# Modulation columns in twos, the first chunk's layer norm in a chained order, a pair's down weights one tile sooner: a two-layer trunk on one core

## The chip, the cores and the metric

The kernel runs on one core of one Trainium2 chip, in one launch. The metric is the device time in microseconds; before the change the median of three runs is 1838.02 us (1836.39 to 1839.01). The profile is of one further execution. Five engines work side by side, each through its own list of instructions in order: TensorE (PE in the profile, its weight loads PEld), VectorE (DVE), ScalarE (ACT), GpSimd (POOL) and SyncE (SP), which issues most DMAs. They meet through semaphores only.

## The reference

The trunk has two layers. x is 1024 tokens by 1024 channels, float32; D_FF is 2816.

```python
def conformer_conv(h, w1, b1, w_dw, b_dw, ln_g, ln_b, w2, b2):
    u = h @ w1 + b1
    a, g = jnp.split(u, 2, axis=-1)
    u = a * jax.nn.sigmoid(g)
    u = lax.conv_general_dilated(u, w_dw...)          # causal, width 31, each channel by itself
    u = jax.nn.silu(layer_norm(u + b_dw, ln_g, ln_b))
    return u @ w2 + b2
...
def reference(x, c, ...):
    c_act = jax.nn.silu(c)
    for i in range(DEPTH):                            # 2
        mod = c_act @ ada_w[i] + ada_b[i]
        sh_m, sc_m, g_m, sh_f, sc_f, g_f = jnp.split(mod, N_ADA, axis=-1)
        h = modulate(rms_norm(x, norm_mix_g[i]), sh_m, sc_m)
        y = conformer_conv(h, ...) if i == 0 else multiscale_pool(h, ...)
        x = x + (1.0 + g_m)[:, None, :] * y
        h = modulate(rms_norm(x, norm_ffn_g[i]), sh_f, sc_f)
        y = (silu(h @ w_gate) * (h @ w_up)) @ w_down
        x = x + (1.0 + g_f)[:, None, :] * y
    return rms_norm(x, final_g)
```

multiscale_pool takes, for each of four groups of 256 channels, the trailing mean over 2, 4, 8 or 16 tokens minus the token itself, and then a 256 x 256 product.

## The kernel before

x lies transposed, 128 channels on the partitions, in eight tiles (k = 0 to 7) of two chunks of 512 tokens, A (`ch.i` 0) and B. Each float32 product is made of three matmuls: weights and activations are split into a high part (`hi`, a cast to a shorter mantissa) and the rest (`lo`), and hi·hi, lo·hi and hi·lo are summed in PSUM. A "product" below is one such matmul, 128x128 by 128x512. For a weight tile SP loads `raw`; ScalarE casts it to its high half (`CAST w<-raw`) and writes its negative (`ACTIVATE w<-raw`), and GpSimd issues a second DMA that adds the weight from memory onto the latter (`POOL DMA_DIRECT2D w<-in_...`), which leaves the low half. A tile of 128x1024 serves 24 products (8 k times 3).

The order of the instructions on the engines is set while the program is written out. The products come in units (`unit`, `run_units`), and between them a planner (`pace`) advances tasks, which are Python generators, as far as an estimated clock of TensorE allows: a `yield "load"` holds a task back for `LOAD["load"]` us of TensorE's time, and `stretch[0]` scales the estimated times of VectorE and GpSimd. So a number in these tables moves instructions of all engines.

The stages: start-up until 68 us; until 244 us the conv input products `a` and `g` of A, then of B. Meanwhile VectorE and ScalarE with GpSimd do the 31 taps of the depthwise convolution (`ca` on VectorE, `pr` on ScalarE and `pa` on GpSimd), ScalarE squares x of chunk B (`acc<-x`, `t<-x`) for its norm, and the task `ada_columns` makes the modulation's columns j = 2 to 5: 32 tiles `adaw` of 512 KB, in two buffers (`ADA_BUFS`), each used by four small matmuls `ada`. From 228 to 258 us stands the layer norm with silu of A: `mean` on TensorE, subtraction and squares, `var` on TensorE, a reciprocal root in twelve small VectorE instructions (`var`, `col`), `rstd` on TensorE (it spreads the root over the partitions), then for each k a multiplication by rstd (VectorE), silu (ScalarE, into `t`), the cast `vhi` and the rest `vlo`, which the products `y` of conv_out read. Then the FFN of layer 0. The pool mixer of layer 1 (`pool_mixed`: window sums `win`, halves `mxhi` and `mxlo`) runs beside FFN products, at about 960 to 1010 us for one chunk and 1340 to 1380 us for the other. In each of three FFN stretches (from about 780, 1156 and 1523 us) `ffn_mixed` uses pairs: class `Pair` makes sums of two weight tiles, class `Downs` fetches the down weights (`raw<-in_wdn_dram`) of the tiles before. ScalarE and VectorE need a `raw` tile before a pair's products can start.

The list `before` of `ffn_mixed` holds the units that run ahead of the pairs, and the planner walks it in order.

Of the kernel before, what the change touches and what calls it, by code (L numbers as in the profile page):

```python
# [9 lines left out]
F32 = mybir.dt.float32  # L10
# [9 lines left out]
KT = D // P  # L20
# [17 lines left out]
ADA_BUFS = 2  # L38
# [8 lines left out]
PHTAPS = 29  # L47
PHLEN = 135
OUT_B = 3
LOAD = {"load": 2.5, "slow": 18.0, "next": 4.0}  # L50
AHEAD = 4
STRETCH = 1.35
LATER = 300
WARM = (22, 10, 6)
# [58 lines left out]
def trunk(ctx, tc, xT, c, vec, ada, adan, w1, w2, wgu, wdn, wpl, wph, out):  # L113
# [37 lines left out]
    def either(n):  # L151

        now = clock["PE"]
        v, g = (max(clock[e], now) + engines[e].price("tensor_tensor", n) for e in "VG")
        return V_ if v <= g else G_
# [13 lines left out]

    tasks = []  # L170
    lax = [False]
    stretch = [1.0]
    forced = [False]

    def step(t, e):
# [61 lines left out]
    def slot(ch, name, dt=F32R):  # L237

        return slots.tile([P, ch.n], dt, tag=f"s{ch.i}", name=nm(name))
# [22 lines left out]
    def temp(n, name="t", bufs=0):  # L262
        t = tmp.tile([P, TMPW], F32, tag=name if bufs else "t", name=nm(name), bufs=bufs or 4)
        return t[:, :n]
# [47 lines left out]
    def ada_load(src):  # L312
        w = raws.tile([P, D], F32, tag="ada", name=nm("adaw"), bufs=ADA_BUFS)
        sync.dma_start(w, src)
        return w
# [43 lines left out]
    def ada_columns(js):  # L359


        todo = [(j, k) for j in js for k in range(KT)]
        src = lambda j, k: adan[k, :, (j - 2) * D : (j - 1) * D]
        ws = [ada_load(src(*t)) for t in todo[:ADA_BUFS]]
        for i, (j, k) in enumerate(todo):
            yield "load"
            if k == 0:
                acc = bank("ada")
            w = ws.pop(0)
            for g in range(4):  # L370
                matmul(acc[32 * g : 32 * g + 32, :Q], ccols[:, k, :], w[:, g * Q : g * Q + Q], start=k == 0, stop=k == KT - 1)
            clock["PE"] -= 1.3
            if i + ADA_BUFS < len(todo):
                ws.append(ada_load(src(*todo[i + ADA_BUFS])))
            if k == KT - 1 and (j == 2 or not held[0]):
                yield from columns_done(j, acc)
            elif k == KT - 1:
                held_back.append((j, acc))
# [348 lines left out]
    def centred(vs, mean, n):  # L727
# [7 lines left out]
                V_.tensor_tensor(vs[k], vs[k], mean, op=SUB)  # L735
        yield

    def layer_norm_silu(ch):

        n = ch.n  # L740
        vs = [st["u", ch.i, k][:, HALO:] for k in range(KT)]
        acc = temp(n, "acc", 2)
        for k in range(1, KT):
            while not (st["taps", ch.i][k - 1] and st["taps", ch.i][k]):
                yield "wait"
            V_.tensor_tensor(acc, vs[0] if k == 1 else acc, vs[k], op=ADD)
            yield
        yield "stats"
        b = bank("mean")
        matmul(b, ones, acc, start=True, stop=True)  # L750
        if ch.i == 0:
            yield from centred(vs, b, n)
        else:
            for k in range(KT):
                V_.tensor_tensor(vs[k], vs[k], b, op=SUB)
                yield
        acc = yield from sum_sq([vs[k] for k in CENTRED], n)
        rstd = yield from mean_rsqrt(acc, n)
        S_.activation(tmp.tile([P, 16], F32, tag="col0", name=nm("col"), bufs=1)[:, 0:1], acc[:, 0:1], AF.Silu)
        hv = [(slot(ch, "vhi"), slot(ch, "vlo")) for _ in range(KT)]  # L760
        for k in range(KT):
            V_.tensor_tensor(vs[k], vs[k], rstd, op=MUL)
            sw = temp(n)
            S_.activation(sw, vs[k], AF.Silu, bias=V("conv_ln_b", k), scale=V("conv_ln_g", k))
            hi, lo = hv[k]
            if ch.i == 0 and k % 2 == 0:
                V_.tensor_copy(hi, sw)
            else:
                S_.copy(hi, sw)
            (either(n) if ch.i else (G_, V_)[k % 2]).tensor_tensor(lo, sw, hi.bitcast(F32), op=SUB)  # L770
            yield
        st["v", ch.i] = hv

# [47 lines left out]
    def pool_mixed(ch, k):  # L821

        w = WINDOWS[k // (KT // len(WINDOWS))]
        h = st["hp", ch.i][k]
        n = ch.n
        end = PHALO + n
        bufs = [window(end, "win") for _ in range(2 if w > 2 else 1)]
        cur, have, i = h, 1, 0
        while have < w:
            first = PHALO - (w - 2 * have)  # L830
            nxt = bufs[i % 2]
            either(n).tensor_tensor(nxt[:, first:end], cur[:, first:end], cur[:, first - have : end - have], op=ADD)
            cur, have, i = nxt, have * 2, i + 1
            yield
        f = PHALO
        if ch.i == 0:
            f = PHALO + w - 1
            head = cur[:, PHALO:f]
            G_.tensor_tensor(head, head, recip[:, : w - 1], op=MUL)
            G_.tensor_tensor(head, head, h[:, PHALO:f], op=SUB)  # L840
        V_.scalar_tensor_tensor(cur[:, f:end], cur[:, f:end], 1.0 / w, h[:, f:end], op0=MUL, op1=SUB)
        hi, lo = st["mx", ch.i, k] = slot(ch, "mxhi"), slot(ch, "mxlo")
        S_.copy(hi, cur[:, PHALO:end])
        yield
        V_.tensor_tensor(lo, cur[:, PHALO:end], hi.bitcast(F32), op=SUB)

# [288 lines left out]
    def ffn_mixed(ch, l, until, at_end=False):  # L1135

        before = []
        for f in range(0, PLAIN, 2):
            before += [ffn_p1(ch, l, f, True, False), ffn_p1(ch, l, f + 1, True, False)]
            if f:  # L1140
                before.insert(-1, ffn_p2(ch, l, [f - 2, f - 1], True))
        mates = [Pair(ch, l, f, which) for f in range(PLAIN, until, 2) for which in range(2)]
        mine, theirs = [None] * len(mates), []
        for i, f in enumerate(range(PLAIN - 2, until - 2, 2)):
            first, second = Downs(ch, l, (f, f + 1), (0, 1)), Downs(ch, l, (f, f + 1), (2, 3))
            for at, d in ((2 * i + 1, first), (2 * i + 2, second)):
                if at < len(mates):
                    mine[at] = d
                else:
                    theirs.append(d)  # L1150
        last, = theirs
        paired = [(lambda take: mates[0].prepare(), ())]
        for i, me in enumerate(mates):
            if i + 1 == len(mates):
                paired.append((lambda take: reserve.__setitem__(0, 2), ()))
            paired.append(ffn_pair(ch, l, me, mates[i + 1] if i + 1 < len(mates) else None, mine[i], (mine + [last])[i + 1]))
        paired.append((lambda take: last.load(last.dps[1]), ()))
        rest = ffn(ch, l, True, at_end, until, ffn_p2(ch, l, [until - 2, until - 1], True))
        rest[1:1] = [alone(last)]
        return before, paired, rest  # L1160
# [388 lines left out]
```

## Time and profile before

| | us |
| --- | --- |
| median of 3 runs | 1838.02 (1836.39 to 1839.01) |
| the profiled execution | 1835.9 |
| its span | 1834.0 |
| TensorE busy | 1784.8 |
| VectorE busy | 1310.7 |
| ScalarE busy | 1040.0 |
| GpSimd busy | 587.8 |

In the tables below, `out<-in` names what an instruction writes and reads, `x8` how many instructions a row groups, and `[7.76 <-DMA adaw<-in_adan_dram]` says that the engine stood idle for 7.76 us ahead of it until that DMA was done. Rows begin with their start in us and their length. In a table by stretch the columns are the length, then busy time with number of instructions for TensorE, its weight loads, VectorE, ScalarE and GpSimd, then TensorE's granted clock, the DMA engines' share and GB/s.

### The profile page before, as it was taken

What the parts mean: (1) busy time and instruction counts of PE and PEld (TensorE: products, weight loads), DVE (VectorE), ACT (ScalarE), POOL (GpSimd) and SP (SyncE); (2) the same over time, 40 slices, a digit from 0 to 9 for tenths busy, and PEclk for the clock granted to TensorE, in tenths of its full rate; (3) what the DMA queues carried; (4) which work ended last, traced back from release to release, by engine and by line L of the source; (5) the groups of instructions that cost most, each with busy time, mean ns of one, the idle gap of its engine ahead of it and who ended that gap; (6) DMA issues with size and microseconds to landing.
All of it is one profiled execution on the core that took longest, in us unless ns stands there. A gap on an engine that the chain in (4) does not pass through costs nothing.

```text
span 1834.0 us, 26261 instructions
## 1 busy us (share of the span) xinstructions
PE 1784.8 (97%) x9748; PEld 1519.4 (83%) x9748; DVE 1310.7 (71%) x2123; ACT 1040.0 (57%) x1609; POOL 587.8 (32%) x631
## 2 busy tenths in 40 slices
PE   8899989999999999999999999999999999999997
PEld 7666678888888887889997888999988889999986
DVE  8779855988866237889978448778684468887845
ACT  3566666776657455555555455555555546555543
POOL 2579732877843111311116121111151211011111
PEclk9899999999999999999999999999999999999998
DMA  8978858888987987977766877655568776655562
GB/s 273 294 213 234 219 124 208 207 232 208 232 212 192 246 216 172 240 215 206 204 182 143 199 171 177 173 139 138 134 138 218 173 177 164 181 142 136 133 143 70
DMA packets 115953, 342.73 MB, mean 187 GB/s; under 512 B 11505, under 2 KB 21873, under 8 KB 115826
## 3 DMA queue, kind: packets, MB, share of 16 engines
q1 hardware_dynamic: 76944, 223.60, 36.4%
q0 software_dynamic: 37728, 116.41, 35.5%
q8 instruction: 76, 1.25, 0.3%
q10 hardware_dynamic: 1154, 1.05, 0.2%
q14 instruction: 51, 0.42, 0.1%
HBM read 336.83 MB, written 4.19 MB: 186 GB/s over the span
## 4 chain that ended last, share of the span: by engine, by line
PE 82%; DVE 7%; DMA 5%; issue 2%; ACT 2%; POOL 1%; SPq 0%; POOLq 0%; ACTq 0%; DVEq 0%
PE dn L129 22%; PE gate L129 22%; PE up L129 22%; PE y L129 6%; PE a L129 3%; PE g L129 3%; DVE adaw L107 2%; DMA adaw<-in_adan_dram 2%; DMA raw<-in_wgu_dram 2%; DVE t L107 1%; DMA w<-in_wdn_dram 1%; DMA w<-in_wgu_dram 1%; DVE x L107 1%; PE ada L129 1%; ACT w L107 1%
## 5 line engine op out<-in xcount | busy, mean ns | idle before, releaser
L129 PE MATMUL dn<-ghi,w 128*128 128x512 f32 (+1 forms) x1440 | 469.9, 389 | 2.5 <-DMA w<-in_wdn_dram 1.1
L107 ACT ACTIVATE w<-raw 128x1024 fp32r<-128x1024 f32 (+1 forms) x262 | 243.0, 928 | 329.5 <-PE dn L129 97.4
L107 ACT CAST w<-raw 128x512 fp32r<-128x512 f32 (+1 forms) x392 | 322.1, 824 | 134.2 <-PE up L129 53.5
L107 DVE SCALAR_TENSOR_TENSOR x<-dn,gains,x 128x512 f32<-128x512 f32 (+1 forms) x360 | 262.9, 734 | 81.5 <-PE dn L129 78.6
L129 PE MATMUL gate<-hhi,w 128*128 128x512 f32 (+1 forms) x1088 | 312.9, 361 | 3.8 <-DMA w<-in_wgu_dram 3.7
L129 PEld LDWEIGHTS dn<-ghi,w 128*128 128x128 f32 x1440 | 269.2, 188 | 56.2 <-DMA w<-in_wdn_dram 2.0
L129 PE MATMUL up<-hhi,w 128*128 128x512 f32 (+1 forms) x1088 | 310.2, 358 | 0.0
L129 PE MATMUL dn<-glo,w 128*128 128x512 f32 (+1 forms) x720 | 279.3, 388 | 0.9 <-POOL glo L107 0.9
L107 POOL TENSOR_TENSOR pa<-pa,pr 128x512 f32<-128x512 f32 x168 | 229.3, 1418 | 23.5 <-ACT pr L107 20.5
L129 PEld LDWEIGHTS gate<-hhi,w 128*128 128x128 f32 x1088 | 197.9, 190 | 36.3 <-DMA w<-in_wgu_dram 4.5
L1009 POOL DMA_DIRECT2D w<-in_wgu_dram x80 | 69.6, 870 | 493.9 <-ACT w L107 161.9
L129 PEld LDWEIGHTS up<-hhi,w 128*128 128x128 f32 x1088 | 196.7, 189 | 30.5
L129 PE MATMUL gate<-hlo,w 128*128 128x512 f32 (+1 forms) x544 | 196.0, 360 | 1.4 <-DVE hlo L107 1.4
L129 PE MATMUL up<-hlo,w 128*128 128x512 f32 (+1 forms) x544 | 194.6, 358 | 0.0
L409 POOL DMA_DIRECT2D w<-in_wgu_dram x96 | 86.2, 898 | 322.1 <-ACT w L107 298.3
L107 DVE TENSOR_TENSOR t<-t,up 128x512 f32<-128x512 f32 (+1 forms) x88 | 55.0, 625 | 170.4 <-PE up L129 157.7
L107 DVE SCALAR_TENSOR_TENSOR ca<-u,vecs,ca 128x512 f32<-128x512 f32 x252 | 174.1, 747 | 0.7
L129 PEld LDWEIGHTS dn<-glo,w 128*128 128x128 f32 x720 | 136.1, 189 | 24.0 <-POOL glo L107 1.2
L107 ACT ACTIVATE pr<-u,vecs 128x512 f32<-128x512 f32 x168 | 113.2, 716 | 15.9 <-POOL pa L107 6.2
L129 PEld LDWEIGHTS gate<-hlo,w 128*128 128x128 f32 x544 | 103.4, 190 | 18.3 <-DVE hlo L107 2.3
L129 PEld LDWEIGHTS up<-hlo,w 128*128 128x128 f32 x544 | 102.7, 189 | 15.5
L107 DVE TENSOR_TENSOR w<-raw,w 128x512 fp32r<-128x512 f32 (+1 forms) x123 | 85.6, 704 | 32.5 <-ACT w L107 29.4
(190 smaller groups left out, 3373.1 us busy)
## 6 DMA issues: line engine op xcount, KB each, us to landing
raw<-in_wgu_dram SPq DMA_DIRECT2D x176, 512.0 KB, 5.1
w<-in_wgu_dram POOLq DMA_DIRECT2D x96, 512.0 KB, 8.1
raw<-in_wdn_dram SPq DMA_DIRECT2D x88, 512.0 KB, 5.6
adaw<-in_ada_dram SPq DMA_DIRECT2D x64, 512.0 KB, 5.9
w<-in_wdn_dram POOLq DMA_DIRECT2D x48, 512.0 KB, 8.5
raw<-in_w_dram SPq DMA_DIRECT2D x44, 512.0 KB, 6.6
w<-in_wgu_dram POOLq DMA_DIRECT2D x80, 256.0 KB, 5.6
w<-in_w_dram POOLq DMA_DIRECT2D x34, 512.0 KB, 8.3
```

The costliest lines, as they stand in the source:

```text
L107: self.last = self.order(getattr(self.eng, name)(out, *args, **kw))
L129: last_mm[0] = nc.tensor.matmul(out, lhsT, rhs, start=start, stop=stop, **kw).ins.name
L409: order(nc.gpsimd.dma_start(as_src(lo), src, accum_op=ADD))
L1009: order(nc.gpsimd.dma_start(lo, src, accum_op=ADD))
```

## The change

1. `ada_columns` takes two tiles at a time: eight `ada` matmuls stand together, the next two loads are issued together behind them, and the task is held back 4.8 us instead of 2.5 ahead of each two (11 us ahead of the first).
2. Until the norm of A before its FFN, `stretch` is 1.06 instead of 1.0.
3. For chunk A, `silu_in_order` replaces the loop over k: the VectorE instructions are chained as multiplications 0 and 1, then for each k the cast (even k) and the rest (odd k and k = 0) and the multiplication of k + 2. Before, the planner let all eight multiplications go first.
4. In `pool_mixed` the cast to `mxhi` moves from ScalarE to VectorE.
5. In `ffn_mixed` the fetch of the first pair's down weights goes one unit ahead of where the pair would make it.

```diff
-LOAD = {"load": 2.5, "slow": 18.0, "next": 4.0}
+LOAD = {"load": 4.8, "late": 11.0, "slow": 18.0, "next": 4.0}
+STRETCH_FRONT = 1.06
...
-    stretch = [1.0]
+    stretch = [STRETCH_FRONT]
...
         for i, (j, k) in enumerate(todo):
-            yield "load"
+            if i % ADA_BUFS == 0:
+                yield "load" if i else "late"
...
-            if i + ADA_BUFS < len(todo):
-                ws.append(ada_load(src(*todo[i + ADA_BUFS])))
+            if i % ADA_BUFS == ADA_BUFS - 1:
+                ws += [ada_load(src(*t)) for t in todo[i + 1 : i + 1 + ADA_BUFS]]
...
+    def silu_in_order(vs, rstd, hv, n):
+        last = [None]
+        def chained():
+            if last[0] is not None:
+                tc.add_manual_dep(V_.last.ins, last[0], edge, reason="as the products take them")
+            last[0] = V_.last.ins.name
+        def scaled(k):
+            V_.tensor_tensor(vs[k], vs[k], rstd, op=MUL)
+            chained()
+            sw = temp(n)
+            S_.activation(sw, vs[k], AF.Silu, bias=V("conv_ln_b", k), scale=V("conv_ln_g", k))
+            return sw
+        ahead = [scaled(0), scaled(1)]
+        for k in range(KT):
+            sw = ahead.pop(0)
+            hi, lo = hv[k]
+            if k % 2 == 0:
+                V_.tensor_copy(hi, sw)
+                chained()
+            else:
+                S_.copy(hi, sw)
+            if k % 2 or k == 0:
+                V_.tensor_tensor(lo, sw, hi.bitcast(F32), op=SUB)
+                chained()
+            else:
+                G_.tensor_tensor(lo, sw, hi.bitcast(F32), op=SUB)
+            if k + 2 < KT:
+                ahead.append(scaled(k + 2))
+            yield
...
+        if ch.i == 0:
+            yield from silu_in_order(vs, rstd, hv, n)
...
-        S_.copy(hi, cur[:, PHALO:end])
+        V_.tensor_copy(hi, cur[:, PHALO:end])
...
+        before.insert(-1, (lambda take: mine[1].fetch(), ()))
```

The order of the instructions at three places. First SP from 64 us on, where the loads of the columns (`adaw`) and of the conv weights (`raw`) are issued; before:

```order
46 L139 DMA adaw_105_647<-in_adan_dram 128x1024
47 L404 DMA raw_158_826<-in_w1_dram 128x1024
48 L139 DMA adaw_106_649<-in_adan_dram 128x1024
49 L404 DMA raw_164_837<-in_w1_dram 128x1024
50 L404 DMA raw_183_980<-in_w1_dram 128x1024
51 L404 DMA raw_189_991<-in_w1_dram 128x1024
52 L139 DMA adaw_116_684<-in_adan_dram 128x1024
53 L139 DMA adaw_124_722<-in_adan_dram 128x1024
```

and now:

```order
48 L140 DMA adaw_106_649<-in_adan_dram 128x1024
49 L406 DMA raw_157_802<-in_w1_dram 128x1024
50 L406 DMA raw_176_943<-in_w1_dram 128x1024
51 L406 DMA raw_182_954<-in_w1_dram 128x1024
52 L406 DMA raw_289_1586<-in_w1_dram 128x1024
53 L406 DMA raw_292_1593<-in_w1_dram 128x1024
54 L140 DMA adaw_161_830<-in_adan_dram 128x1024
55 L140 DMA adaw_162_832<-in_adan_dram 128x1024
```

Two more raw tiles go ahead of the third and fourth column tiles. On TensorE the first `ada` stands at row 212 before and at row 260 now, and from there two tiles at a time; nine of the sixteen twos stand 24 products behind the two before them.

Second, ScalarE behind the four sigmoids `t<-first`, at about 69 us; `w_103` and `w_104` are the two halves of the third conv weight tile. Before:

```order
38 L107 ACTIVATE pr_111_660<-u_94_616,vecs_76 128x512
39 L107 CAST w_103_642<-raw_102_640 128x1024
40 L107 ACTIVATE w_104_643<-raw_102_640 128x1024
41 L107 CAST w_108_653<-raw_107_651 128x1024
42 L107 ACTIVATE w_109_654<-raw_107_651 128x1024
43 L107 ACTIVATE acc_117_686<-x_1_0_85 128x512
```

and now:

```order
38 L108 ACTIVATE acc_115_679<-x_1_0_85 128x512
39 L108 ACTIVATE pr_111_660<-u_94_616,vecs_76 128x512
40 L108 ACTIVATE pr_116_681<-u_94_616,vecs_76 128x512
41 L108 ACTIVATE t_117_684<-x_1_1_86 128x512
42 L108 ACTIVATE pr_118_687<-u_94_616,vecs_76 128x512
43 L108 CAST w_103_642<-raw_102_640 128x1024
44 L108 ACTIVATE w_104_643<-raw_102_640 128x1024
```

The two squares and two of the taps stand ahead of the halves of that weight.

Third, the layer norm of A, on ScalarE ahead of the silus (`t<-u`); before:

```order
198 L107 ACT_TABLE_LOAD
199 L107 ACTIVATE col_401_2245<-acc_380_2118 128x1
200 L107 ACTIVATE w_432_2316<-raw_430_2313 128x1024
201 L107 CAST w_440_2383<-raw_439_2381 128x1024
202 L107 ACTIVATE t_418_2264<-u_94_616,vecs_76 128x512
```

and now:

```order
199 L108 ACT_TABLE_LOAD
200 L108 ACTIVATE col_409_2264<-acc_381_2132 128x1
201 L108 ACTIVATE w_407_2255<-raw_405_2252 128x1024
202 L108 ACT_TABLE_LOAD
203 L108 ACTIVATE t_401_2242<-g_395_2168,vecs_76 128x512
204 L108 CAST w_441_2385<-raw_440_2383 128x1024
205 L108 ACT_TABLE_LOAD
206 L108 ACTIVATE t_426_2283<-u_94_616,vecs_76 128x512
```

and on VectorE now, inside the root:

```order
271 L108 TENSOR_SCALAR col_400_2230<-col_400_2230 128x4
272 L108 TENSOR_TENSOR var_399_2224<-var_399_2224,col_400_2230 128x4
273 L108 SCALAR_TENSOR_TENSOR u_393_2165<-a_394_2167,vecs_76,t_401_2242 128x512
274 L108 SCALAR_TENSOR_TENSOR var_399_2224<-var_399_2224,col_400_2230 128x4
275 L108 SCALAR_TENSOR_TENSOR col_400_2230<-var_399_2224,col_400_2230 128x4
```

The sigmoid of a product `g` of chunk B (row 203) stands between two loads of ScalarE's tables, where it came behind the silus before, and its product with `a` (row 273) stands between two steps of the root. On TensorE, 48 products stand between `mean` and `var` in both kernels; the 12 that stood between `var` and `rstd` now stand ahead of `mean`, and `rstd` follows `var` at once.

More of the change, by code (lines that the diff above doesn't have):

```diff
@@ L760, in layer_norm_silu @@
         hv = [(slot(ch, "vhi"), slot(ch, "vlo")) for _ in range(KT)]
+        if ch.i == 0:
+            yield from silu_in_order(vs, rstd, hv, n)
+            st["v", ch.i] = hv
+            return
         for k in range(KT):
@@ L765, in layer_norm_silu @@
             hi, lo = hv[k]
[L766 to L770, printed above, removed]
+            S_.copy(hi, sw)
+            either(n).tensor_tensor(lo, sw, hi.bitcast(F32), op=SUB)
             yield
```

## The prediction

> **What bounds the kernel now.** I read the page first (share of each engine), then TensorE's waits, then TensorE's timeline at the long waits, then busy time by stretch. The page's first row:
>
> ```profile
> PE 1784.8 (97%) x9748; PEld 1519.4 (83%) x9748; DVE 1310.7 (71%) x2123; ACT 1040.0 (57%) x1609; POOL 587.8 (32%) x631
> ```
>
> TensorE is busy for 1784.8 of 1834.0 us. The diff takes no product away, so it can gain only from the 49.2 us in which TensorE stands still, and from the stretches in which it runs at a lower clock. Those 49 us, by what ended each wait:
>
> ```profile
> PE ada L129 <- DMA adaw<-in_adan_dram: 11.2, 4, 7.8
> ...
> PE y L129 <- DVE vhi L107: 5.3, 1, 5.3
> PE gate L129 <- DMA w<-in_wgu_dram: 3.7, 2, 3.1
> ...
> PE gate L129 <- ACT t L107: 2.6, 1, 2.6
> ...
> PE y L129 <- POOL vlo L107: 0.9, 1, 0.9
> ```
>
> The columns are total, times, longest. Four edits of the diff stand at four of these rows: the modulation columns (11.2), the layer norm of chunk A (5.3 and 0.9), the pool stage (3.1 of the 3.7), the first pair (2.6). Together 23.1 us lie in reach (11.2 + 5.3 + 0.9 + 3.1 + 2.6). TensorE's timeline at these places, and the clock in the stretches around them:
>
> ```profile
> 85.91 1.08 PE L129 MATMUL ada<-adaw,ccols 128*32 128x256 f32 x8 [7.76 <-DMA adaw<-in_adan_dram]
> ...
> 228.04 1.02 PE L129 MATMUL mean<-acc,ones 128*128 128x512 f32 x2
> ...
> 249.79 0.80 PE L129 MATMUL y<-vhi,w 128*128 128x512 f32 x1 [5.30 <-DVE vhi L107]
> ...
> 1007.58 1.22 PE L129 MATMUL gate<-hhi,w 128*128 128x512 f32 x2 [3.12 <-DMA w<-in_wgu_dram]
> ...
> 80.00:100.00 20.00, 14.09 (x69) 8.97 (x69) 14.69 (x23) 11.72 (x17) 15.04 (x14) 0.74 0.85 236
> 160.00:180.00 20.00, 20.00 (x150) 15.10 (x143) 19.06 (x24) 12.17 (x19) 17.25 (x16) 1.00 0.85 246
> 245.00:260.00 15.00, 9.28 (x29) 7.11 (x30) 10.38 (x17) 10.29 (x15) 6.29 (x5) 0.77 0.35 73
> 1007.00:1014.00 7.00, 6.42 (x16) 5.03 (x17) 2.17 (x4) 3.03 (x4) 1.15 (x2) 0.52 1.07 263
> ```
>
> In the last four rows the clock is the number behind the five engines, then the DMA share and GB/s. The waits of 7.76, 5.30 and 3.12 us are each followed by a low clock (0.74, 0.77, 0.52), and the 20 us without one keep 1.00. A mean of 0.52 over the 7 us from 1007 means that nearly all of them, some 6 us of matmuls, ran at half speed: 3 us are lost beside the wait. I price a lost clock at 3 us each time. The Trainium skill ("TensorE: Matmul & The Clock Gate", Part 1: what's actually happening) puts the drop behind an idle window of about 3.4 us and the return behind as long a busy one. By that a lost clock would be about 1.7 us, and the pool stage below 0.7 us less; the trace differs, with a drop after 3.12 us and some 6 us of low clock.
>
> **The columns in twos.** A tile's matmuls interrupt the products; TensorE's rows around one tile, and the time that the 32 tiles took to land:
>
> ```profile
> 211.36 0.39 PE L129 MATMUL a<-hhi,w 128*128 128x512 f32 x1
> 211.68 0.64 PE L129 MATMUL ada<-adaw,ccols 128*32 128x256 f32 x8
> ...
> 212.58 0.39 PE L129 MATMUL g<-hlo,w 128*128 128x512 f32 x1
> 212.81 0.63 PE L129 MATMUL g<-hhi,w 128*128 128x512 f32 x2
> ...
> DMA to landing us min/median/max: 3.5/5.4/14.1
> ```
>
> A product takes 0.23 us (212.58 to 212.81; 0.227 over longer stretches). From the last product ahead of a tile to the second behind it are 1.22 us (211.36 to 212.58) instead of 2 x 0.23, so one tile costs about 0.77. Two together I estimate at 1.2, since the turn to another shape and back is paid once: 0.33 saved sixteen times, 5.3 us (ends 0 and 7). The first tile moves some 45 products back, so its 7.76 us wait goes, and the smaller ones (11.2 - 7.8 = 3.4) lose their cause.
>
> Two things come in their place. First, on ScalarE four squares and taps more now stand ahead of the cast of the raw tile from which GpSimd issues the accumulating load of w_104. The rows that show it before (the last is of the view of DMAs from 70 to 85: count, KB, median us to landing):
>
> ```profile
> 69.98 1.07 ACT L107 CAST w<-raw 128x1024 fp32r<-128x1024 f32 x1
> ...
> 73.77 0.61 ACT L107 ACTIVATE acc<-x 128x512 f32<-128x512 f32 x1
> ...
> 72.34 1.04 POOL L409 DMA_DIRECT2D w<-in_w_dram  x1 [0.63 <-ACT w L107]
> ...
> w<-in_w_dram POOLq DMA_DIRECT2D x3, 512.0 KB, 9.6
> ```
>
> Four operations of the 0.61 us kind are some 2.2 us: the load goes out near 74.5 instead of 72.3 and lands, at 9.6, near 84.1. TensorE stands at the first tile's place at 71.0 in both kernels; w_104 is first read 40 products behind it in the new order, at 71.0 + 40 x 0.227 = 80.1. That is a new wait of 4.0 us, with its own clock loss; before, this landing was hidden below the 7.76 us wait. (Ends: 0 if it lands like a median adaw tile, in 5.4 us; 6 if it takes 11.5, what is left of the 14.1 once the raw tiles are out of the way.)
>
> Second, nine of the sixteen pairs stand only 24 products behind the one before. With two buffers both loads are issued when the pair before has been read and are wanted 24 x 0.227 = 5.4 us later, just the median landing of a single tile. Such a stretch of 5.4 + 1.2 = 6.6 us must move four tiles of 0.52 MB (two of columns, one raw, one accumulating): 2.1 MB. By the 160:180 row a full DMA share moves 246 / 0.85 = 289 GB/s, which takes 7.2 us: 0.6 late. On the other side, that row itself held the same bytes with TensorE at 20.00 of 20 us, no wait: 0. I take 0.5, nearer the bytes, since two loads at once leave no room to shift: 9 x 0.5 = 4.5. (Upper end: see the first rival.)
>
> The mean on TensorE then comes at 228.0 + 2.7 (twelve products moved ahead of it) - 11.2 - 5.3 + 4.0 + 4.5 = 222.7. VectorE must have the taps' sum by then. Its rows before, and its longest cause of idle time from 64 to 229:
>
> ```profile
> 75.57 0.70 DVE L107 TENSOR_TENSOR acc<-acc,t 128x512 f32<-128x512 f32 x1 [5.05 <-ACT t L107]
> ...
> 226.26 1.42 DVE L107 TENSOR_TENSOR acc<-acc,u 128x512 f32<-128x512 f32 x2
> ...
> DVE u L107 <- ACT t L107: 12.6, 6, 4.7
> ```
>
> It ended at 227.7, right ahead of the mean, so it must come sooner too. The squares that moved ahead on ScalarE take away most of the 5.05, and the 12.6 are waits for sigmoids, that is for products, which come sooner by what TensorE gains. The first alone gives 223, with half of the second 216: it doesn't clearly decide, but it lies close.
>
> **The layer norm.** The order shows 48 products between mean and var in both kernels, but before, twelve more cover the root; now none do. The rows of the root:
>
> ```profile
> 240.80 0.17 DVE L107 TENSOR_SCALAR var<-var 128x4 f32<-128x4 f32 x1 [1.48 <-PE var L129]
> ...
> 244.53 4.87 DVE L107 TENSOR_TENSOR u<-u,rstd 128x512 f32<-128x512 f32 x8 [1.35 <-PE rstd L129]
> 249.32 0.42 DVE L107 CAST vhi<-t 128x512 fp32r<-128x512 f32 x1
> ...
> 255.63 1.28 ACT L107 ACT_TABLE_LOAD   x1
> 256.92 0.69 ACT L107 ACTIVATE t<-g,vecs 128x512 f32<-128x512 f32 x1
> ```
>
> Before, all eight multiplications (4.87) run ahead of the first cast. In the chained order only two do, with one silu: cast after about 0.6 + 0.7 + 0.4 (the last two from the rows at 256.92 and 249.32) instead of 4.87 + 0.4, some 3.5 us sooner. But two things step in. A sigmoid stands on ScalarE between two table loads, so the silu's table is loaded again behind the first multiplication, 1.28 us; and the fifth row of the root on VectorE is now a product that waits for that sigmoid, up to 1 us plus its own 0.7. So of the 3.5 us some 0.2 to 0.5 are left: nothing, with ends of -1.5 and +3.5. Mean to y stays near 21.5 us, against 249.8 - 228.0 = 21.8 (48 products and the root in both), and y starts at 222.7 + 21.5 = 244.2, 5.6 us sooner. The clock loss behind it stays. The Trainium skill ("ScalarE: Activation LUTs", What ACT_TABLE_LOAD costs) gives 1.28 us for the load, as in the row, and a drain of 1.38 beside it. By that the two extra switches would cost 2.8 us more than I count, and the time would be 1831; but the row behind the load starts at its end (256.92 after 255.63 + 1.28), so the trace shows no drain here, and I give that case no chance apart from the forecast's own width.
>
> **The pool stage.** The wait of 3.12 us is for an accumulating load that ScalarE releases late, behind a cast of mxhi:
>
> ```profile
> 996.39 0.62 ACT L107 CAST mxhi<-win 128x512 fp32r<-128x512 f32 x1 [3.82 <-DVE win L107]
> 996.92 1.05 ACT L107 ACTIVATE w<-raw 128x1024 fp32r<-128x1024 f32 x1
> ...
> 998.38 0.90 POOL L409 DMA_DIRECT2D w<-in_wgu_dram  x1 [1.16 <-ACT w L107]
> ...
> 990.00:995.00 5.00, 5.00 (x23) 4.08 (x22) 5.00 (x7) 0.62 (x1) 3.50 (x6) 1.00 0.03 7
> ```
>
> With that cast on VectorE, the weight's own step (996.92) waits for nothing but its slot, and the DMA goes out at 995.5 to 997 (GpSimd has three more window sums ahead of it). It landed 9.2 us after issue, so TensorE waits 0 to 2 instead of 3.1, and perhaps keeps its clock: 1.4 + half of 3, about 3 us. Against it: VectorE was full (5.00 of 5.00, the third busy number) and gets 8 x 0.42 = 3.4 us more a stage. So -1 to +4.6; the x updates that free TensorE's banks keep their places, hence +3. In the second pool stage 0.5 us at most can go; I take 0.4.
>
> **The pair's down weights** one tile sooner: SP issues the raw down tile ahead of a gate tile. The rows:
>
> ```profile
> 773.10 0.39 SPq L1030 DMA_DIRECT2D raw<-in_wdn_dram  x1
> 773.58 0.42 SPq L963 DMA_DIRECT2D raw<-in_wgu_dram  x1
> ...
> 784.63 0.62 ACT L107 CAST w<-raw 128x512 fp32r<-128x512 f32 x1 [0.69 <-DMA raw<-in_wgu_dram]
> ...
> 786.09 0.39 PE L129 MATMUL gate<-thi,shi 128*128 128x256 f32 x1 [2.62 <-ACT t L107]
> ```
>
> ScalarE's step ahead of the copy for which TensorE waits ends with the tile issued at 773.58; that tile is still waited for, only less crowded: 0 to 2.6, half, 1.3. The other two places show no wait on TensorE before, so nothing to gain.
>
> **Sum.** 5.6 + 3 + 0.4 + 1.3 = 10.3. The profiled execution took 1835.9 us (span 1834.0 and 1.9 around it), 2.1 below the median; 10 us off the median of 1838.0 give 1828.
>
> **Rivals.** *Slower: the pairs come late.* Both loads of a pair are issued together once the pair before has been read, 6.6 us ahead of use. If the two need longer than a median single tile (5.4), TensorE waits nine times. 1.1 us more than my 0.5 eats the whole sum (9 x 1.1 = 10); slower by over 0.2% it gets from 2.05 us a pair, a landing at 7.5 us. The 14.1 us landing speaks for it, the median against. At 2.2 us: 9 x 1.7 - 10.3 = +5, about 1843.
> *Given back.* The mean is held by VectorE's taps or by pairs at 1.1 us, and the front gives nothing: 3 + 0.4 + 1.3 less a little for the fuller VectorE in the pool stage, about 1834.
> *More.* w_104 lands in time (no 4.0), its clock loss and that at 1007 vanish too: 10.3 + 4.0 + 3 + 1.5 = 18.8, about 1819.
> *The pairs don't pair*, a tile in twos costing 2 x 0.77: 5.3 less, about 1833, counted with given back.
>
> **Chances.** The forecast (1824 to 1832) 0.45, more 0.14, given back 0.30 (of which 0.17 within 0.2%), slower 0.11. 0.2%, 3.7 us, is about what a measurement of this kernel can tell from no change. So faster 0.72, same 0.17, slower 0.11. The range goes from 1819 (half of "more" below it) to 1838.5 (the slower case above it).
>
> **What would show it.** In the profile after: the first wait for an adaw tile gone and one for w of about 4 us near 80; the mean near 223; y near 244 with a wait of over 5 us for vhi; pairs with waits of 0.5; three table loads around the silus; at the gate in the pool stage a wait below 2 us with the clock at 1.00. I'm wrong if the pairs wait over 1 us each, or if w_104 isn't waited for.

## The result, and the profile after

The changed kernel takes 1840.58 us (median of 15 runs, 1836.68 to 1843.97) against 1836.94 (15 runs) of the kernel before: a ratio of 1.0024 [1.0016, 1.0033], slower by some 4 us. The forecast was 10 us faster. The profiled execution took 1843.57 us, with a span of 1841.4; it lies 3.0 above its median, and that of before 1.0 below its own, so the two traces are 7.4 us apart where the medians are 3.6 apart.

The page's first row of the changed kernel: TensorE does the same work as before, and VectorE 7.4 us more.

```profile
PE 1784.8 (97%) x9748; PEld 1523.5 (83%) x9748; DVE 1318.1 (72%) x2136; ACT 1036.2 (56%) x1598; POOL 590.5 (32%) x634
```

TensorE's waits in the changed kernel (total, times, longest):

```profile
PE ada L130 <- DMA adaw<-in_adan_dram: 14.7, 10, 6.9
PE rstd L130 <- DVE col L108: 10.8, 5, 4.4
PE gate L130 <- DMA w<-in_wgu_dram: 4.6, 2, 2.9
PE y L130 <- DVE vhi L108: 3.4, 1, 3.4
...
PE mean L130 <- DVE acc L108: 1.7, 1, 1.7
PE a L130 <- DMA w<-in_w_dram: 1.5, 1, 1.5
```

The columns wait longer than before (14.7 against 11.2). The wait for vhi is shorter (3.4 against 5.3), but that for rstd, which comes ahead of it in the layer norm, has grown from 6.7 to 10.8. The 2.6 us of the first pair are gone. TensorE's timeline at these places:

```profile
82.29 0.73 PE L130 MATMUL a<-hhi,w 128*128 128x512 f32 x2 [1.51 <-DMA w<-in_w_dram]
98.77 1.08 PE L130 MATMUL ada<-adaw,ccols 128*32 128x256 f32 x8 [6.93 <-DMA adaw<-in_adan_dram]
101.34 1.08 PE L130 MATMUL ada<-adaw,ccols 128*32 128x256 f32 x8 [1.50 <-DMA adaw<-in_adan_dram]
...
237.60 1.13 PE L130 MATMUL mean<-acc,ones 128*128 128x512 f32 x2 [1.68 <-DVE acc L108]
...
254.84 2.08 PE L130 MATMUL rstd<-ident,col 128*128 128x128 f32 x8 [4.40 <-DVE col L108]
260.34 0.79 PE L130 MATMUL y<-vhi,w 128*128 128x512 f32 x1 [3.43 <-DVE vhi L108]
...
1011.56 0.73 PE L130 MATMUL gate<-hhi,w 128*128 128x512 f32 x2 [1.69 <-DMA w<-in_wgu_dram]
...
1380.67 0.94 PE L130 MATMUL gate<-hhi,w 128*128 128x512 f32 x2 [2.88 <-DMA w<-in_wgu_dram]
```

Against the kernel before, mean is 9.6 us later (1.1 of it are there at the first product `a`, at 69.29 against 68.23) and y 10.6. At the gate of the first pool stage it is 4.0: of the 6.6 won back, the pair gave 2.6 and the shorter wait at this gate 1.4. At the gate of the second it is 3.5, although the wait there has grown by 2.3, and behind it the lost clock and a wait for down weights bring it to 7 at the end. So the front loses ten, the middle wins most of it back, and the second pool stage loses again. The same stretches of the changed kernel (last three columns: clock, DMA share, GB/s):

```profile
64.00:80.00 16.00, 16.00 (x72) 13.21 (x72) 12.59 (x18) 14.71 (x21) 8.31 (x12) 1.00 0.72 243
80.00:100.00 20.00, 11.41 (x62) 7.09 (x60) 10.71 (x17) 15.95 (x23) 16.71 (x16) 0.86 1.03 273
100.00:120.00 20.00, 18.51 (x96) 13.54 (x96) 10.48 (x25) 6.30 (x9) 5.66 (x7) 0.80 0.56 162
140.00:160.00 20.00, 18.54 (x129) 11.86 (x130) 17.73 (x27) 10.56 (x16) 16.86 (x21) 0.91 0.75 214
...
1376.00:1384.00 8.00, 5.12 (x17) 3.75 (x17) 5.15 (x9) 2.61 (x3) 1.53 (x2) 0.81 1.01 214
```

In the front there are three stretches below full clock: 20 x (0.14 + 0.20 + 0.09) = 8.6 us of clock are missing, against 20 x 0.26 = 5.2 in the kernel before. What falls on an idle TensorE costs nothing: behind the waits some 5.4 us are left (0.56 from 98.77 to 109.00, without the wait inside it, and 0.76 from 140 to 147), against 3.1 before (0.56 from 85.91 to 93.00). The DMA share is 0.72 where it was 0.87 before (64 to 80), and 1.03 right after. The SP queue of the changed kernel shows why:

```profile
62.85 0.33 SPq L140 DMA_DIRECT2D adaw<-in_adan_dram  x1
...
66.27 0.42 SPq L140 DMA_DIRECT2D adaw<-in_adan_dram  x1
67.03 17.03 SPq L406 DMA_DIRECT2D raw<-in_w_dram  x5
85.49 0.89 SPq L140 DMA_DIRECT2D adaw<-in_adan_dram  x2
...
DMA to landing us min/median/max: 3.7/6.9/15.4
```

Both buffers of the columns are full early and stay so until the first two tiles are read, behind 60 products. The loads of the second two go out at 85.49, together with a burst of weights, and land 13 and 15 us later.

### The profile page after: what moved, and what is told of

Same layout as the page of the kernel before. It is cut to its first block, busy times and chain, and to the rows that moved or that the text cites. A ratio compares the mean times of both kernels' runs of the same rounds, so it can differ in the third digit from the quotient of the medians.

```text
span 1841.4 us, 26271 instructions
## 1 busy us (share of the span) xinstructions
PE 1784.8 (97%) x9748; PEld 1523.5 (83%) x9748; DVE 1318.1 (72%) x2136; ACT 1036.2 (56%) x1598; POOL 590.5 (32%) x634
## 3 DMA queue, kind: packets, MB, share of 16 engines
q10 hardware_dynamic: 1154, 1.05, 0.2%
## 4 chain that ended last, share of the span: by engine, by line
PE 81%; DVE 7%; DMA 6%; issue 2%; POOL 2%; ACT 1%; SPq 0%; POOLq 0%; ACTq 0%; DVEq 0%
PE gate L130 23%; PE up L130 23%; PE dn L130 22%; PE y L130 6%; DMA adaw<-in_adan_dram 3%; PE a L130 2%; PE g L130 2%; DVE adaw L108 1%; DVE t L108 1%; DMA w<-in_wdn_dram 1%; DMA w<-in_wgu_dram 1%; DVE win L108 1%; PE ada L130 1%; DVE x L108 1%; DVE hlo L108 1%
## 5 line engine op out<-in xcount | busy, mean ns | idle before, releaser
L108 POOL TENSOR_TENSOR pa<-pa,pr 128x512 f32<-128x512 f32 x171 | 235.0, 1437 | 33.7 <-ACT pr L108 31.0
```

Of the source, the lines that this page charges most:

```text
L108: self.last = self.order(getattr(self.eng, name)(out, *args, **kw))
```

## The experiments

**Each part alone.** The chained layer norm alone (the function `silu_in_order` and its call, nothing else):

```diff
+        if ch.i == 0:
+            yield from silu_in_order(vs, rstd, hv, n)
```

> The kernel before with the chained order of the layer norm of A alone. Theory (the chain itself is good, and what spoiled it in the changed kernel is the sigmoid and the table loads that the longer estimates of the front put in the root): rstd to the first vhi cast takes about 1.8 us instead of 4.8, y starts near 246.5 instead of 249.8 with a wait near 2 us, the clock stays at 1.00 behind it: 3 to 6 us faster than before, 1832 to 1834. Rival (the chain itself makes VectorE and ScalarE wait for each other): y starts late all the same or waits at each k, within 2 us of before.

1832.38 us against 1837.18: 0.9978 [0.9967, 0.9988], faster by 4. VectorE, TensorE and the stretch of this kernel, with no low clock:

```profile
243.79 1.28 DVE L107 TENSOR_TENSOR u<-u,rstd 128x512 f32<-128x512 f32 x2 [1.34 <-PE rstd L129]
245.42 0.43 DVE L107 CAST vhi<-t 128x512 fp32r<-128x512 f32 x1 [0.34 <-ACT t L107]
...
245.90 0.50 PE L129 MATMUL y<-vhi,w 128*128 128x512 f32 x1 [2.15 <-DVE vhi L107]
...
245.00:260.00 15.00, 12.87 (x50) 9.11 (x51) 9.20 (x17) 11.21 (x16) 3.92 (x4) 1.00 0.34 69
```

From the first multiplication to the cast 1.63 us pass instead of 4.79, as worked out; and a wait of 2.15 in place of 5.30 keeps the clock. So the chain is good by itself. In the changed kernel the same place reads (ScalarE, then VectorE):

```profile
257.72 1.28 ACT L108 ACT_TABLE_LOAD   x1 [4.26 <-DVE u L108]
...
252.55 0.75 DVE L108 SCALAR_TENSOR_TENSOR u<-a,vecs,t 128x512 f32<-128x512 f32 x1 [1.30 <-ACT t L108]
...
259.86 0.43 DVE L108 CAST vhi<-t 128x512 fp32r<-128x512 f32 x1 [1.62 <-ACT t L108]
```

The root stands still for 1.30 us for the sigmoid, and the table for the silus is loaded only when the first multiplication is done, after ScalarE has been idle for 4.26 us: var to y takes 10.9 us where it takes 6.8 in the kernel with the chain alone.

The columns in twos alone (`ada_columns` and `LOAD` of the change, the estimates not stretched):

> The kernel before with the columns in twos alone (load 4.8, late 11.0; the estimates not stretched). Theory (the twos lose more to late loads than they save): a wait of 6 to 8 us at the second two near 97, waits of 0.5 to 1.3 at most later ones, mean 4 us later than the 228.0 of before: 3 to 6 us slower, near 1841. Rival (the twos save their 0.27 us sixteen times, and it is the stretched estimates that cost): 2 to 5 us faster, near 1833.

1844.82 us: 1.0041 [1.0027, 1.0055], slower by 7.6; mean at 239.9. This part alone costs twice what the whole change costs. What twos save is as worked out, though. TensorE's rows around two tiles that are there in time, in the changed kernel:

```profile
111.20 0.39 PE L130 MATMUL a<-hhi,w 128*128 128x512 f32 x1
111.52 1.07 PE L130 MATMUL ada<-adaw,ccols 128*32 128x256 f32 x16
...
112.86 0.40 PE L130 MATMUL a<-hlo,w 128*128 128x512 f32 x1
```

111.20 to 112.86 is 1.66, less 0.46 for two products is 1.20: 0.34 saved at each two.

The cast of mxhi on VectorE alone, and then in the second pool stage only:

```diff
-        S_.copy(hi, cur[:, PHALO:end])
+        V_.tensor_copy(hi, cur[:, PHALO:end])                              # alone
+        (V_.tensor_copy if ch.i == 1 else S_.copy)(hi, cur[:, PHALO:end])  # second stage only
```

> The kernel before with the mxhi cast on VectorE alone. Theory (GpSimd's own window sums wait for the fuller VectorE and hold the accumulating load that ScalarE now releases sooner): first pool stage as before (wait about 3 us at the gate, clock lost), second stage a wait of 2 to 3 us instead of 0.55 with a clock loss, 3 to 5 us slower, near 1841. Rival (the prediction's: the load goes out sooner): the first wait below 2 us with the clock kept, the second gone, 3 us faster, near 1834.

> The kernel before with the mxhi cast on VectorE in the second pool stage only. Theory (there GpSimd's window sums wait for the fuller VectorE and hold the accumulating load for the gate): wait of 2 to 3 us at that gate instead of 0.55 and a clock loss, 2 to 4 us slower, near 1840. Rival (the loss in the second stage came from what the first had moved): no wait above 1 us there, within 1 us of before.

Both stages: 1835.00 us, 0.9991 [0.9981, 1.0001], unclear and at most 3.5 us faster. The second only: 1839.73 us, 1.0013 [1.0003, 1.0023], slower by 0.6 to 4. The kernel with both, at the gates, then ScalarE and GpSimd ahead of the second:

```profile
1006.06 0.73 PE L129 MATMUL gate<-hhi,w 128*128 128x512 f32 x2 [1.41 <-DMA w<-in_wgu_dram]
...
1376.30 0.73 PE L129 MATMUL gate<-hhi,w 128*128 128x512 f32 x2 [2.89 <-DMA w<-in_wgu_dram]
...
1361.16 1.06 ACT L107 ACTIVATE w<-raw 128x1024 fp32r<-128x1024 f32 x1 [9.02 <-PE dn L129]
...
1367.54 1.06 POOL L107 TENSOR_TENSOR win<-hp 128x526 f32<-128x526 f32 x1 [1.62 <-DVE mxlo L107]
1368.54 0.89 POOL L409 DMA_DIRECT2D w<-in_wgu_dram  x1
```

ScalarE has the weight ready at 1362.2 instead of 1368.4, 6 us sooner, but GpSimd issues its DMA only at 1368.54 (before: 1369.05), behind a window sum that waits for VectorE's mxlo. TensorE came to this gate 3.3 us sooner than before (it waits from 1373.41 on, against 1376.67), so for it the DMA is late. The kernel with the cast in the second stage only, which is as before up to there, shows it plainly: its DMA goes out at 1371.37, 2.3 us later than before, and the wait at the gate is 2.30 instead of 0.55:

```profile
1378.55 0.74 PE L129 MATMUL gate<-hhi,w 128*128 128x512 f32 x2 [2.30 <-DMA w<-in_wgu_dram]
```

What was taken off ScalarE's queue came back on GpSimd's, and more. So the theory's reading of the second stage holds, but it was wrong about the first: in the kernel with both, the wait fell to 1.41 us and the clock stayed at 1.00, with the DMA issued at 999.03, no sooner than before (998.38); it landed in 7.0 us instead of 9.2. The trace suggests why: ScalarE, done earlier, frees its `raw` tiles, and SP issues the next two (the pool weights) at 993.49 instead of 998.00. They move while the DMA engines were nearly idle before (0.03 from 990 to 995), and from 998 to 1001, beside the load for the gate, the DMA share is 0.44 instead of 0.69. No run tests this alone.

The earlier fetch alone:

> The kernel before with the earlier fetch of the pair's down weights alone. Theory: the 2.62 us wait of the first pair near 786 is gone and nothing else moves: 2.6 us faster, near 1834.5. Rival (the gate tile behind it is late in turn, so that the wait only changes its name): within 1 us of before.

1834.21 us, 0.9986 [0.9975, 0.9997]: 2.6 us faster, and its trace has no wait at the first pair any more.

The stretched estimates alone (`stretch = [1.06]`), and the changed kernel without them:

> The kernel before with the estimates of the front stretched to 1.06 alone. On TensorE the twelve products between var and rstd move ahead of mean; the table loads stay as before. Theory (the root's cover is worth what it hides only if mean isn't later for it; the products ahead of mean delay it by 2.7 us): y starts 0 to 1 us later than 249.8 and the idle time in the root grows by 2.7: 0 to 3 us slower, near 1838. Rival (the stretch is the whole of what the changed kernel loses beyond its parts): 4 us slower, near 1841.

> The changed kernel with the estimates of the front not stretched (1.0 instead of 1.06). Theory (the stretch moved the twelve products from the root to ahead of mean, and the sigmoid with two table loads into the root): var to y is 3 to 4 us shorter than the 10.9 of the changed kernel, rstd without a wait of over 1 us, and the time is about the sum of the parts alone (-4.8 + 7.6 - 2.2 - 3.0): 1834 to 1837. Rival (the parts hinder each other for another reason): 1840 as the changed kernel.

Alone: 1843.20 us, 1.0038 [1.0025, 1.0052], 6 to 7 us slower, more than the rival's 4. Here 24 more products stand ahead of mean, 5.4 us (I had counted twelve, which is right for the changed kernel only), and the layer norm doesn't get shorter by having fewer behind it:

```profile
235.67 1.10 PE L129 MATMUL mean<-acc,ones 128*128 128x512 f32 x2 [0.98 <-DVE acc L107]
246.63 1.05 PE L129 MATMUL var<-ones,acc 128*128 128x1 f32 x8 [1.66 <-DVE acc L107]
...
257.60 0.80 PE L129 MATMUL y<-vhi,w 128*128 128x512 f32 x1 [5.30 <-DVE vhi L107]
```

mean to y is 21.9 us, with 36 products below it, against 21.75 with 60 before. Taken out of the changed kernel, 1839.19 us and 1.0011 [1.0000, 1.0023] remain, 1.4 us less by the medians, with an interval that overlaps that of the changed kernel. var to y is 6.8 us there, 4 less, as expected, but the forecast of 1834 to 1837 was too low: the columns wait 21.0 us in place of 14.7, with 4.11 at 177.22 and 3.28 at 197.46, where none of the changed kernel's is longer than 1.34 behind the second two. So the stretched estimates spoil the chain and, in the changed kernel, ease the later twos; how they do the latter no run separates. The ratios of the five parts alone multiply to 1.0034, against 1.0024 [1.0016, 1.0033] measured together, which is as near as such intervals can tell.

**Why the twos cost.** Two theories: the loads of two tiles are too late with two buffers at this spacing, or the first two, held back with full buffers, waste the DMA engines. First the spacing (twos alone, held back 7.5 us, the first 2.5), and the first two early (4.8, the first 2.5):

```diff
-LOAD = {"load": 4.8, "late": 11.0, "slow": 18.0, "next": 4.0}
+LOAD = {"load": 7.5, "late": 2.5, "slow": 18.0, "next": 4.0}   # wide
+LOAD = {"load": 4.8, "late": 2.5, "slow": 18.0, "next": 4.0}   # early
```

> The kernel before with the columns in twos alone, held back 7.5 us ahead of each two and 2.5 ahead of the first, so that most twos stand 36 products behind the two before instead of 24 and the first stands where the first single tile stood. Theory (a pair's two loads start only when the pair before has been read, and 24 products, 5.4 us, are shorter than the 6.6 us in which a load lands): the waits at the later twos go, the 0.34 us saved at each two is left, 2 to 5 us faster than before, near 1833. Rival (the bytes are too many for the DMA engines whenever two tiles come at once): waits of 0.5 us and more stay at most twos, slower than before, near 1840.

> The kernel before with the columns in twos alone, held back 4.8 us ahead of each two but only 2.5 ahead of the first. It tells the late first two from the narrow spacing. Theory (both cost): the first stall is one wait near 86 of 6 to 9 us as in the kernel before, w isn't waited for near 82, later twos still wait 0.5 us and more: 1838 to 1842, between before and the 1844.8 of the twos held back 11 us. If the late first two was all: near 1832. If the spacing was all: 1844 again.

Wide: 1855.91 us, 1.0107 [1.0089, 1.0125], 20 us slower where 2 to 5 faster was expected. Between 91 and 227 its twos wait 0.25 us in all, so the spacing was the cause of the later waits; but the columns then last too long:

```profile
227.50 2.04 PE L129 MATMUL mean<-acc,ones 128*128 128x512 f32 x2 [7.76 <-DVE acc L107]
251.46 1.08 PE L129 MATMUL ada<-adaw,ccols 128*32 128x256 f32 x8 [7.52 <-DMA adaw<-in_adan_dram]
```

The last two tiles stand inside the root and wait for their DMA, and mean waits for VectorE. Early: 1841.33 us, 1.0023 [1.0009, 1.0036], between before and the twos with the late first two, as expected; the old stall is back at 85.54 with 7.88 us.

That mean waited for VectorE made me think that the taps hold it whatever the columns do. The kernel before, with one column tile loaded once and read 32 times; it leaves out the other 31 loads, so its columns are not those of the reference:

> The kernel before, but all 32 steps of the modulation columns read one tile that is loaded once, so 31 loads of 0.5 MB are left out and the columns are not the reference's; the matmuls stay, one tile at a time. It shows what the front could gain at most if no column tile were ever late. Theory (VectorE's taps hold the mean: it was waited for until 227.5 where TensorE came sooner): TensorE's 11.2 us of waits and the clock loss go, but mean waits for acc of VectorE and stands at 222 to 227, so 2 to 6 us faster than before, near 1832. Rival (the prediction's: the taps come sooner as the products do): mean at 213 to 217, 11 to 15 us faster, near 1823.

1821.09 us, 0.9920 [0.9907, 0.9933]: 15 us faster (16 by the medians). The theory fell, and the rival's 11 to 15 came true: mean stands at 214.92 with a wait of 1.09 for VectorE, so the taps do follow the products. It is also the worth of the front: some 15 us hang on these loads.

The second theory was tried with the twos alone and in the changed kernel, holding back the second two instead of the first:

```diff
-                yield "load" if i else "late"
+                yield "late" if i == ADA_BUFS else "load"
```

> The kernel before with the columns in twos, the second two held back 11 us instead of the first (4.8 ahead of the others). On TensorE only the first two moves: 24 products behind the start of conv_in instead of 60. Theory (held back with full buffers, the first two kept the next loads from starting until 85.5): the loads of the second two start near 76, land before 97, their waits of 3.9 and 2.1 us go with the clock loss near 100; later waits stay as in the twos held back at the first: 6 to 9 us faster than its 1844.8, near 1837. Rival (two tiles at a time are late by themselves): 1843 to 1845.

> The changed kernel with the second two held back 11 us instead of the first. Theory (as in twos_second): the waits of 6.9 and 1.5 us near 99 go with their clock loss, mean and y come 8 to 11 us sooner than in the changed kernel, near 1831. Rival (two tiles at a time are late by themselves): 1840.

The twos alone: 1840.28 us, 1.0017 [1.0002, 1.0033], some 4.5 us less than with the first two held back, where 6 to 9 were expected, and still no faster than before; their columns wait 12.6 us in all. The changed kernel: 1834.43 us, 0.9986 [0.9974, 0.9998]; it turns from slower to faster by one condition, some 6 us, though less than the 9 expected. SP, TensorE and the stretches of the latter:

```profile
75.48 0.34 SPq L140 DMA_DIRECT2D adaw<-in_adan_dram  x1
...
78.78 0.33 SPq L140 DMA_DIRECT2D adaw<-in_adan_dram  x1
...
84.58 0.74 PE L130 MATMUL a<-hhi,w 128*128 128x512 f32 x2 [2.85 <-DMA w<-in_w_dram]
101.89 0.64 PE L130 MATMUL ada<-adaw,ccols 128*32 128x256 f32 x8 [1.70 <-DMA adaw<-in_adan_dram]
...
64.00:80.00 16.00, 16.00 (x83) 12.52 (x82) 10.26 (x15) 14.71 (x21) 8.00 (x11) 1.00 0.74 271
80.00:100.00 20.00, 17.15 (x90) 13.14 (x88) 18.58 (x34) 18.13 (x27) 18.48 (x17) 1.00 1.05 288
```

The second two's loads start 10 and 7 us sooner and its waits of 6.93 and 1.50 are gone (the row at 101.89 is the third two's); the stretch from 80 has its full clock, and 271 instead of 243 GB/s move from 64 to 80. What stays is the waits of 0.2 to 2 us at later twos (9.5 us in all), and the wait for w has grown from 1.51 to 2.85.

**Combinations.** The chain, the fetch and the cast on VectorE in the first pool stage; the same with single tiles, the third held back 10 us (`yield "late" if i == 2 else "load"`); and the same with twos, the second held back:

> The kernel before with the chained layer norm, the earlier fetch, and the mxhi cast on VectorE in the first pool stage only. Theory (the cast on VectorE helps the first pool stage by 1.7 us of wait and 2.8 of clock, and costs the second 2.3 of wait and a clock loss): no wait above 2 us at either gate, 10 to 12 us faster than before, near 1826. Rival (the first stage gained only since what stood ahead of it had moved): 7 to 8 us faster, near 1829.5, with 3 us of wait at the first gate.

> The combination of the chained layer norm, the earlier fetch and the cast on VectorE in the first pool stage, with the third column tile (and so all behind it) held back 10 us instead of 2.5. Theory (its load lands 11 us after issue because five raw and accumulating tiles land with it; 24 products more ahead of it cover that): the 7.7 us wait near 86 shrinks below 3 us, the clock is kept, w is waited for 1 to 2 us near 82; since the taps hold the mean, only 0 to 4 us faster than the combination's 1827.9, near 1826. Rival (the wait only moves to the next column tile): 1828 to 1831.

> The combination (chained layer norm, earlier fetch, cast on VectorE in the first pool stage) with twos, the second two held back 11 us. Against the same combination with single tiles held back at the third (1819.2). Theory (the 5.4 us that the twos save at the turns of shape go into waits of 0.5 us and more at the later twos, with only two buffers): no faster than the single tiles, 1819 to 1826. Rival (the twos are worth their 5.4 us once the start is right): 1814 to 1817.

1827.88 us, 0.9951 [0.9937, 0.9965], 9 us faster; 1819.24 us, 0.9913 [0.9898, 0.9928], 16 us faster (18 by the medians), beyond the 0 to 4 that I expected of it over the first; and with twos 1829.98 us, 0.9959 [0.9946, 0.9972], slower than the 1819 to 1826 that I expected. Single tiles, held back at the right one, beat twos by 8 to 11 us. The kernel of 1819 (its profiled execution took 1824.57):

```profile
96.53 0.64 PE L129 MATMUL ada<-adaw,ccols 128*32 128x256 f32 x8 [1.55 <-DMA adaw<-in_adan_dram]
...
223.25 1.02 PE L129 MATMUL mean<-acc,ones 128*128 128x512 f32 x2
...
80.00:100.00 20.00, 17.82 (x96) 12.54 (x94) 20.00 (x36) 17.81 (x25) 18.91 (x18) 1.00 1.04 303
```

No long wait and no lost clock from 80 to 100, and VectorE, which stood still for 9.3 of these 20 us in the changed kernel, is busy throughout.

## Why the prediction was wrong

The sum put y at 244.2; it came at 260.34 in the trace, 16.1 later. By its steps:

- **The first tile moved back, "so its 7.76 us wait goes"**: this failed, and it is the largest miss. I followed the tile that moved, but not its buffer: with both buffers full until that tile is read, the next loads wait as well. The order in the text on the change shows the two loads behind two more raw tiles, and I didn't follow that row to its landing. The stall came back at the second two with 8.4 us, none of which stood in the sum. With the second two held back instead, these waits go and the kernel is some 6 us faster. That kernel still takes 1834.43 us where 1828 was forecast, so the rest of the sum was some 6 us too good as well.
- **w_104 late by 4.0**: right in kind, but it measured 1.5: the load went out later than I thought (76.4) but landed within 6 us instead of 9.6. It was waited for on its own, not in place of the other.
- **The clock loss "stays"**: behind rstd and y it did (3.1 us of clock missing before, 3.3 after). In the front, where the sum left it as it was, it grew from 3.1 to 5.4 us behind the waits.
- **Nine narrow twos at 0.5**: somewhat low; the later twos wait 6.3 us in all against 4.5. 0.34 saved at each two was right too.
- **The taps, 216 to 223**: mean waited 1.7 for them at 237.6. They follow the products, as the kernel with one tile shows, but lose what TensorE loses early: VectorE was busy for 10.71 of the 20 us from 80 on.
- **The layer norm, "nothing"**: the gain of the chain (3.2 us, with the clock kept), the table load behind the first multiplication (1.28) and the sigmoid in the root (var to rstd takes 5.35 us instead of 3.62, so 1.7) came about as priced, and yet mean to y came at 22.7 against 21.5. I had seen that TensorE has no product left inside the root, but not priced it: it waits 4.40 us there, its clock falls to 0.50, and rstd takes 2.08 us instead of 1.05. The edit behind this, as behind the sigmoid, is the stretched estimate: without it var to y is 6.8 us.
- **The sum up to mean** put it at 222.7, and it came 14.9 later. Of these, 8.4 are the stall at the second two, 2.3 the clock, 1.8 the later twos, 1.7 the taps and 1.1 the later start, and w takes 2.5 off: 12.8. The other 2 us I can't place.
- **The first pool stage, +3**: about right (with the cast alone 1.7 us of wait and the lost clock are gone), but not by the mechanism; the DMA was issued no sooner. **The second, +0.4**: wrong in sign, the named danger ("VectorE was full") was put in the wrong stage.
- **The pair, 1.3**: the upper end, 2.6.
- **The rivals**: slower was given 0.11 and a mechanism of late twos. That was the right place, but I priced it by the landing of a regular two, not by the first that starts late.

The Trainium skill's drain of 1.38 us behind a table load ("ScalarE: Activation LUTs", What ACT_TABLE_LOAD costs) isn't seen after either: the silu starts at 259.01, right behind 257.72 + 1.28.

## What to carry to other kernels

When a consumer is held back, look at its buffers: until it reads, the next load can't start, so hold back the consumer whose loads are on their way, not the one whose buffers are full. A release that is moved off one in-order queue (ScalarE's cast) comes sooner only if the queue that issues behind it (GpSimd's DMA) doesn't wait for the engine that took the work. And a number that scales a planner's estimates is an edit of its own: run it alone, and take it alone out of the whole, since here it cost 6 to 7 us alone and undid the part that was worth 4, and yet taking it out of the changed kernel gained only 1.4 us by the medians.

## What the runs showed of the hardware

A table load can carry the wait of the activation behind it: in the changed kernel it came after 4.26 us on an idle ScalarE, when the operand was ready, and then took its 1.28.

The clock is lost in portions. The missing clock of the stretches is 3.4 us (0.52 over 7), 1.7 (0.79 or 0.81 over 8), 1.8 (0.91 over 20) or 5.2 (0.74 over 20): about one, two or three times 1.7. What of it falls into the wait itself costs nothing: of the 5.2, 3.1 lie behind it. How many follow a wait isn't set by its length alone. The wait of 3.12 us at the first gate lost two portions in the kernel before (0.52 over the 7 us from 1007), but one in the kernel with the cast in the second stage only (0.76 over the same 7 us), which has the same wait there. Short waits close together lose one, too: 1.34 and 0.60 us stand ahead of the 0.76 from 140 to 147 in the changed kernel. The changed kernel with the second two held back lost the clock behind 2.17 us, the twos held back early kept it at first behind 3.38 us, and the matmuls of the chain alone kept theirs behind 2.15. TensorE's rows and the stretch of the first of these, then of the second:

```profile
1373.93 1.22 PE L130 MATMUL gate<-hhi,w 128*128 128x512 f32 x2 [2.17 <-DMA w<-in_wgu_dram]
...
1373.00:1381.00 8.00, 7.07 (x24) 5.73 (x25) 2.34 (x4) 1.15 (x3) 0.88 (x1) 0.79 1.05 241
```

```profile
1008.35 0.73 PE L129 MATMUL gate<-hhi,w 128*128 128x512 f32 x2 [3.38 <-DMA w<-in_wgu_dram]
...
1009.85 1.01 PE L129 MATMUL gate<-hhi,w 128*128 128x512 f32 x2
...
1008.00:1016.00 8.00, 7.65 (x26) 6.16 (x27) 1.68 (x3) 3.70 (x5) 0.89 (x1) 0.79 1.06 250
```

The second lost one portion too, but from 1.5 us after the wait's end. So in these runs a single wait above 2 us has to be priced with its clock, with 0 to 3.4 us, and not only by its length.

The Trainium skill ("TensorE: Matmul & The Clock Gate", Part 1: what's actually happening) says that activity is judged in a window of 3.4 us that runs freely, and that the clock is half or full. Portions of 1.7 us, which is 3.4 us at half speed, and their varying place agree with that; the drop behind 2.17 us of idleness is shorter than the window it names, and there the trace decides.
